# Values of both branches made ahead of the projection stream, as two stages of seven block products

## The chip, the cores and the metric

The kernel runs on one core of a Trainium2 chip. The metric is the device time of one execution in microseconds, as the median of the runs shown. All data is float32. The matrix products that matter run as three passes of the "fp32r" kind: each operand is split into a high part and a low part, and high times high, high times low and low times high are added up in PSUM. TensorE is called PE here, VectorE DVE, ScalarE ACT, GpSimd POOL, and the engine that only issues transfers SP.

## The reference

A sequence of 1024 tokens with 1024 channels goes through one layer. What is computed, cut to what matters:

```python
h = rms_norm(x, norm_w) * (1 + scale) + shift          # scale, shift from c @ ada_w
hq, hf, hi, hz, gq, gk, gv, gz, ga, mg = split(h @ w_in)
y_h = hgrn2_branch(hq, hf, hi, hz)                     # 8 heads of 128
y_g = gla_branch(gq, gk, gv, gz, ga)                   # 4 heads, keys 128, values 256
merged = sigmoid(mg0) * (y_h @ w_branch0) + sigmoid(mg1) * (y_g @ w_branch1)
out = rms_norm(x + gate * (merged @ w_out), final_norm_w)
```

Each branch is a gated linear attention in chunks: a head needs its queries, keys, per-channel decays, its values, and a gate z. The values are plain columns of the projection: `gv = h @ w_in[:, C_GV:C_GV+1024]` for the four GLA heads and `hi = h @ w_in[:, C_HI:C_HI+1024]` for the eight HGRN heads. Each of these two is a product of 1024x1024 by 1024x1024, and these two products are what the change rewrites.

## The kernel before

**Staging.** The normalised input h is made transposed, in eight pieces of 128 channels, each split into `h_hi[k]` and `h_lo[k]` (L238 to L242), and h itself is also stored to DRAM (`h_d`). A first group of products (L372, functions `products` and `first_group`) makes the four GLA queries and two of the GLA keys while the second half of h is still being made. Its transposes of x (L227) are the last readers of the tiles that hold x. Then a stream of jobs runs: each job loads one block of w_in columns through SP, splits it (the cast to the high part on ACT, L200, the subtraction for the low part on DVE, L201) and runs its products on PE.

- `Feat` (L581): 128 columns of w_in as the stationary operand, 1024 tokens moving, 48 matmuls of 512 columns. There are 34 of these jobs, for keys, queries, gates and decays.
- `Vblk` (L640 to L642): the values of one GLA head. The tokens are stationary and 256 columns of w_in move: 192 matmuls of 256 columns, four times.
- `Vblk2` (L683 to L685): the values of four HGRN heads, 512 columns moving: 192 matmuls of 512 columns, twice.

**Order of the work.** `Stream.go` runs the jobs; after each step of a job `weave` lets generators on a side track (the attention heads, one after the other) and on a back track (`prepare`, `gate_side`) write their next piece of code. A side generator yields the number of steps that it wants to wait, and PACE is what one step counts on the side track. Once the list of jobs is written this way, a scheduler orders each engine's instructions, so neighbours may change places, but each engine then executes strictly in its order. All large SBUF tiles come from 46 slots of 4 KB a partition (`Slots`); a new tile in a slot waits until the old one's readers are done, a store to DRAM among them.

**What stands around the change.** `alpha_side` makes the decays of the four GLA heads: eight small matmuls (L967) through two PSUM tiles, read by ACT (L969), then exponentials and logarithms on ACT. `factors` (L1198), on the back track, loads the stored h in blocks and makes the four differences of blocks that the later stages need, and stores them (`f_x`). `weight_sums` does the like for later weights. The later stages (`last_stages`, L1387, and `out_stage`, L1564) already multiply in blocks of a two by two split with seven products in place of eight, in the order PRODUCTS. After product 3 of the first of them, `scores_done` and `side_done` wait until the attention heads have written all their code, and take over their PSUM banks.

## Time and profile before

| what | value |
|---|---|
| median of the runs (three, 1207.8 to 1210.91) | 1208.65 us |
| span of the profiled execution (the page gives no time of its own beside it) | 1206.9 us |
| PE busy | 1184.5 us, 98% |
| PEld (weight loads, beside PE) | 988.0 us, 82% |
| DVE busy | 792.9 us, 66% |
| ACT busy | 548.6 us, 45% |
| moved by DMA | 183.51 MB, 152 GB/s over the span |
| last matmuls of the first group start | 111.69 us |
| first value matmul (L640) | 138.05 us |

A busy time is the union of an engine's instructions. Matmuls overlap each other in these records, so the mean duration of one is longer than the distance from one start to the next. The rows of groups give line, engine, operation, names, shape and count, then busy time and mean duration, then the idle time before them and what ended it. The rows of a window give for each engine its busy time and count, then the clock granted to TensorE (1.00 is full), the share of the DMA engines and GB/s.

### The profile page before, as it was taken

To read this page: it belongs to the slowest core of one execution; us is meant where nothing else is said; L and a number is where in the kernel's file an instruction comes from. 1 tells how busy PE (TensorE), PEld (TensorE's weight loads), DVE (VectorE), ACT (ScalarE), POOL (GpSimd) and SP (SyncE) were. 2 spreads that over 40 slices of the span, in tenths; PEclk is the share of its full clock that TensorE was granted. 3 is DMA by queue.
4 is the path that set the end of the run, shared out by engine and by line. 5 is a ranking of instruction groups with operands and counts; after the bars stand their busy time and mean duration, and the time that the engine had idled before them with its cause. 6 is when DMAs were issued, how large, how long until landed. Compare 5 with 4: busy or idle time off the path is not lost.

```text
span 1206.9 us, 20911 instructions
## 1 busy us (share of the span) xinstructions
PE 1184.5 (98%) x8617; PEld 988.0 (82%) x8617; DVE 792.9 (66%) x1258; ACT 548.6 (45%) x798; POOL 94.3 (8%) x204
## 2 busy tenths in 40 slices
PE   6999999999999999999999999999999999999997
PEld 5777889889798888888888888877888888878886
DVE  4737444774857557777965455795654865988994
ACT  5646732434435244234433324455743544444554
POOL 4100000101101012011100000000120000000000
PEclk8999999999999999999999999999999999999999
DMA  9814000754544167354441212154797846435423
GB/s 324 277 70 140 19 19 19 278 154 147 174 141 141 62 218 232 127 167 159 140 166 46 69 53 71 36 175 153 246 344 268 275 152 205 137 105 174 167 100 134
DMA packets 130960, 183.51 MB, mean 152 GB/s; under 512 B 7467, under 2 KB 97633, under 8 KB 130866
## 3 DMA queue, kind: packets, MB, share of 16 engines
q1 hardware_dynamic: 117250, 136.87, 36.0%
q0 software_dynamic: 13568, 45.31, 9.7%
q8 instruction: 67, 1.10, 0.4%
q14 instruction: 27, 0.22, 0.1%
q10 hardware_dynamic: 48, 0.01, 0.0%
HBM read 132.87 MB, written 49.28 MB: 151 GB/s over the span
## 4 chain that ended last, share of the span: by engine, by line
PE 71%; issue 20%; DVE 3%; ACT 2%; DMA 2%; POOL 1%; SPq 0%; POOLq 0%; DVEq 0%; ACTq 0%
PE pd L581 22%; PE pd L1387 13%; PE sc_ps L1387 6%; PE pm L1387 6%; PE pd L1564 3%; PE pd L683 2%; PE pd L684 2%; PE pd L685 2%; PE sc_ps L1564 2%; PE pm L888 2%; PE pm L890 1%; PE pm L869 1%; PE pm L1564 1%; PE sc_ps L723 1%; PE sc_ps L755 1%
## 5 line engine op out<-in xcount | busy, mean ns | idle before, releaser
L581 PE MATMUL pd<-b,b 128*128 128x512 f32 x1632 | 387.8, 394 | 0.0
L581 PEld LDWEIGHTS pd<-b,b 128*128 128x128 f32 x1632 | 302.3, 188 | 65.3 <-issue 1.4
L1387 PE MATMUL pd<-b,b 128*128 128x512 f32 x720 | 173.6, 392 | 1.9 <-DVE b L993 1.0
L1387 PEld LDWEIGHTS pd<-b,b 128*128 128x128 f32 x720 | 133.7, 188 | 32.9 <-PE pd L1387 1.4
L201 DVE TENSOR_TENSOR b<-b,b 128x1024 fp32r<-128x1024 f32 (+1 forms) x86 | 96.2, 1125 | 75.0 <-ACT b L200 59.7
L200 ACT CAST b<-b 128x1024 fp32r<-128x1024 f32 (+1 forms) x86 | 82.5, 971 | 93.2 <-PE pd L581 12.2
L1330 DVE TENSOR_TENSOR b<-b,b 128x1024 fp32r<-128x1024 f32 x56 | 68.5, 1224 | 57.0 <-ACT b L1329 37.0
L1329 ACT CAST b<-b 128x1024 fp32r<-128x1024 f32 x56 | 58.6, 1051 | 66.6 <-PE pd L1387 19.0
L1387 PE MATMUL sc_ps<-b,b 128*128 128x512 f32 x324 | 79.3, 391 | 0.3 <-ACT scT L833 0.3
L640 PE MATMUL pd<-b,b 128*128 128x256 f32 x256 | 74.2, 290 | 0.0
L642 PE MATMUL pd<-b,b 128*128 128x256 f32 x256 | 72.5, 283 | 0.0
L641 PE MATMUL pd<-b,b 128*128 128x256 f32 x256 | 72.4, 283 | 0.0
L1308 DVE TENSOR_TENSOR b<-b,b 128x1024 fp32r<-128x1024 f32 x48 | 57.8, 1222 | 21.8 <-ACT b L1307 14.5
L1387 PE MATMUL pm<-b,b 128*128 128x512 f32 x300 | 72.1, 389 | 0.0
L1387 PEld LDWEIGHTS sc_ps<-b,b 128*128 128x128 f32 x324 | 60.3, 188 | 13.9 <-ACT scT L833 0.7
L1307 ACT CAST b<-b 128x1024 fp32r<-128x1024 f32 x48 | 49.9, 1051 | 35.3 <-PE pd L1387 15.7
L1387 PEld LDWEIGHTS pm<-b,b 128*128 128x128 f32 x300 | 56.3, 188 | 11.7
L372 PE MATMUL pd<-b,b 128*128 128x512 f32 x192 | 52.3, 404 | 2.5 <-ACT b L200 1.5
L775 ACT COPY xb<-b 128x512 f32<-128x512 f32 x48 | 29.4, 620 | 50.5 <-PE sc_ps L755 25.2
L1244 POOL DMA_DIRECT2D ws<-b x64 | 34.7, 542 | 225.4 <-DVE b L1238 121.0
L683 PE MATMUL pd<-b,b 128*128 128x512 f32 x128 | 51.2, 400 | 0.0
L684 PE MATMUL pd<-b,b 128*128 128x512 f32 x128 | 50.0, 390 | 0.0
(300 smaller groups left out, 1955.0 us busy)
## 6 DMA issues: line engine op xcount, KB each, us to landing
b<-in_w_in_dram SPq DMA_DIRECT2D x66, 512.0 KB, 4.0
ws<-b POOLq DMA_DIRECT2D x64, 256.0 KB, 3.0
b<-ws SPq DMA_DIRECT2D x32, 512.0 KB, 4.3
b<-in_x_dram SPq DMA_DIRECT2D x16, 512.0 KB, 6.2
b<-in_ada_w_dram SPq DMA_DIRECT2D x32, 256.0 KB, 6.4
b<-in_w_branch_dram SPq DMA_DIRECT2D x16, 512.0 KB, 4.5
b<-h SPq DMA_DIRECT2D x14, 512.0 KB, 3.8
wo<-b POOLq DMA_DIRECT2D x14, 512.0 KB, 5.3
```

Of the source, the lines that this page charges most:

```text
L200: nc.scalar.copy(hi, src)
L201: nc.vector.tensor_sub(lo, src, hi.bitcast(F32))
L581: nc.tensor.matmul(ps[0:w, th * 512:(th + 1) * 512], a[:, k, 0:w], b[:, th * 512:(th + 1) * 512], start=(k == 0 and n == 0), stop=(k == KT ...
L640: nc.tensor.matmul(o, lh, hi[:, k % 4, :], start=(k == 0), stop=False)
L641: nc.tensor.matmul(o, lh, lo[:, k % 4, :], start=False, stop=False)
L642: nc.tensor.matmul(o, ll, hi[:, k % 4, :], start=False, stop=(k == KT - 1))
L683: nc.tensor.matmul(o, lh, hi[:, k % 2, :], start=(k == 0), stop=False)
L684: nc.tensor.matmul(o, lh, lo[:, k % 2, :], start=False, stop=False)
L1329: nc.scalar.copy(hi, t)
L1330: nc.vector.tensor_sub(lo, t, hi.bitcast(F32))
L1387: nc.tensor.matmul(o, a[:, sl], c, start=(p in (1, 5) and kt == 0 and n == 0), stop=(kt == 3 and n == 2), skip_group_check=True)
L1564: nc.tensor.matmul(o, a, b, start=(p in (1, 5) and kt == 0 and n == 0), stop=(kt == 3 and n == 2), skip_group_check=True)
```

## The change

The 1024x1024 products of the values are taken out of the stream and made right behind the first group, by a new function `front`, in two stages: first the GLA values (s = 0), then the HGRN values (s = 1). Each stage is seven block products of 512x512x512 (order 1, 2, 5, 3, 6, 7, 4), each of which runs over four tiles of 128 tokens with 12 matmuls of 512 columns a tile. The tokens are the stationary operand, the weights move. Four of the products take sums of weight blocks (`v_sums`: loaded, added on DVE, stored, loaded again), and four take the differences of h that `factors` makes, which therefore now run here and no longer on the back track. The results go to DRAM (`v_d`), and each attention head loads its own columns when it comes to its third part (`early`). The GLA queries and keys of the first group are stored too (`qk_d`) and loaded again by each head. `alpha_side` writes its eight matmuls into the first value product. The heads of the GLA branch start behind the gates, PACE is 1.3, and the weight sums start behind the value stages.

```diff
-PACE = 1.1
+PACE = 1.3
...
-        g_state[("q", f) if f < 4 else ("k", f - 4)] = qk_t[f]
...
+                    nc.gpsimd.dma_start(qk_d[f], qk_t[f])
+                    S.free(qk_t[f], sent=True)
...
-    class Vblk:
...
-    class Vblk2:
...
-    def attention(q, k, f, v, vo, V, post, lead=3):
+    def attention(q, k, f, v, V, post, early, lead=3):
...
+        early()
...
+        zs = {}
+        for h in range(4):
+            zb = zs[h] = S.get([T])
+            for th in range(2):
+                pz = mtile()
+                nc.tensor.matmul(pz, aw4[:, h * P:(h + 1) * P], ga4[:, th * 512:(th + 1) * 512],
+                                 start=True, stop=True)
+                nc.scalar.activation(zb[:, th * 512:(th + 1) * 512], pz, AF.Identity,
+                                     bias=vec[:, R_AB + h:R_AB + h + 1])
+            yield 2
+        S.free(ga4, aw4)
...
+            pair = (h0, h0 + 1)
+            for h in pair:
+                m = alphas[h] = S.get([T])
+                nc.vector.tensor_scalar_min(m, zs[h], 0.0)
+                nc.vector.scalar_tensor_tensor(zs[h], m, 2.0, zs[h], ALU.mult, ALU.subtract)
...
+        def early():
+            for i in range(2):
+                v.append(S.get([4, 256]))
+                nc.sync.dma_start(v[i], v_d[0][i * 512:(i + 1) * 512, h * 256:h * 256 + 256].rearrange(
+                    "(c p) f -> p c f", p=P))
...
+        if h < 3:
+            load_qk(h + 1)
...
+    def load_qk(h):
+        for f, key in ((h, "q"), (4 + h, "k")):
+            if f < NG:
+                t = g_state[key, h] = S.get([T])
+                nc.sync.dma_start(t, qk_d[f])
...
+        for vh in range(2):
+            def z_done(ps, h=h, vh=vh):
+                silu_done(g_state, ("z", h, vh))(ps)
+                if vh and h < 3:
+                    start_side(gla_attention(h + 1))
+            J.append(Feat(col(C_GZ + h * 256 + vh * P), rhs_h, z_done))
...
-            while len(S.free_list) < 12:
-                yield 1
...
-    stream.back.append([prepare(), 60])
...
+    def v_sums(s):
+
+        for kk in range(2):
+            y = {}
+            for at_ in ((0, 1), (1, 1), (0, 0), (1, 0)):
+                y[at_] = S.get([2, 512])
+                nc.sync.dma_start(y[at_], w_block(s, *at_, kk))
+            yield
+            e = S.get([2, 512])
+            add = nc.vector.tensor_add
+            add(e, y[0, 1], y[1, 1])
+            add(y[0, 0], y[0, 0], y[0, 1])
+            yield
+            add(y[0, 1], y[0, 0], y[1, 1])
+            nc.vector.scalar_tensor_tensor(y[1, 0], y[0, 1], -1.0, y[1, 0], ALU.mult, ALU.subtract)
+            for p, t in ((5, e), (7, y[0, 0]), (6, y[0, 1]), (3, y[1, 0])):
+                nc.gpsimd.dma_start(vs_d[s][p][kk], t.rearrange("p a f -> p (a f)"))
+            S.free(y[1, 1])
+            S.free(e, y[0, 0], y[0, 1], y[1, 0], sent=True)
+            yield
...
+    def load_vw(n):
+        if n >= len(V_SEQ):
+            return
+        s, p = V_SEQ[n]
+        vraw[n] = []
+        for kk in range(2):
+            t = S.get([2, 512])
+            if p in SUMS:
+                nc.sync.dma_start(t.rearrange("p a f -> p (a f)"), vs_d[s][p][kk])
+            else:
+                nc.sync.dma_start(t, w_block(s, *X_OF[p], kk))
+            vraw[n].append(t)
...
+    def prep_vw(n):
+        if n >= len(V_SEQ):
+            return
+        raw = vraw.pop(n)
+        vw[n] = list(zip(*[split(t) for t in raw]))
+        S.free(*raw)
...
+    def load_xf(n):
+        p = V_SEQ[n][1]
+        xraw[n] = [S.get([T]) for _ in range(2)]
+        for kk in range(2):
+            nc.sync.dma_start(xraw[n][kk], f_x[p][kk])
+
+    def build_xf(n):
+        raw = xraw.pop(n)
+        xf[n] = list(zip(*[split(t) for t in raw]))
+        S.free(*raw)
...
+        def run(self, n):
+            p = V_SEQ[n][1]
+            if p in (1, 5):
+                self.bank[BANK[p]] = RF.get()
+            o = self.bank[BANK[p]]
+            for kt in range(4):
+                x_hi, x_lo = self.x_part(n, kt)
+                w_hi, w_lo = (z[kt // 2][:, kt % 2, :] for z in vw[n])
+                for j, (a, c) in enumerate(((x_hi, w_hi), (x_hi, w_lo), (x_lo, w_hi))):
+                    nc.tensor.matmul(o, a, c, start=(p in (1, 5) and kt == 0 and j == 0),
+                                     stop=(kt == 3 and j == 2), skip_group_check=True)
+                if kt % 2:
+                    stream.weave(1)
...
+        def after(self, p):
+            bank, snap = self.bank, self.snap
+            if p == 1:
+                if self.s:
+                    self.seed()
+                else:
+                    snap[1] = self.take("a", -1.0)
+            elif p == 2:
+                self.put(0, 0, self.take("a"))
+                RF.free(bank.pop("a"))
+            elif p == 5:
+                snap[5] = self.take("e")
+            elif p == 6:
+                t = self.take("b", -1.0)
+                nc.vector.tensor_sub(t, t, bank["e"])
+                self.put(0, 1, t)
+                RF.free(bank.pop("e"))
+            elif p == 7:
+                t = snap.pop(5)
+                nc.vector.tensor_add(t, bank["b"], t)
+                self.put(1, 1, t)
+            elif p == 4:
+                self.put(1, 0, self.take("b"))
+                RF.free(bank.pop("b"))
+
+    def front():
+        vs = [v_sums(s) for s in range(2)]
+        xs = factors(h_d, f_x)
+        for i, _ in enumerate(first_group()):
+            if i == 15:
+                make_ga(1)
+            elif i in (16, 17, 18, 19, 20, 21):
+                next(vs[0])
+            elif i == 22:
+                load_vw(0)
+            stream.weave(1)
+        next(vs[0], None)
+        start_side(alpha_side())
+        lent = [dtile() for _ in range(2)]
+        RF.lend([sc_ps[:, 0:512], sc_ps[:, 512:1024]])
+        RF.lend([pd[:, i * 512:i * 512 + 512] for pd in lent[::-1] for i in range(2)])
+        next(xs)
+        prep_vw(0)
+        load_vw(1)
...
+        def pm_done():
+            while not alpha_ps[0]:
+                stream.weave(1)
+            pms.extend(mtile() for _ in range(2))
+            RF.lend(pms)
+            for i in (2, 3):
+                tiles[0, i].seed()
...
+        for n, i, steps in ((0, 1, 2), (0, 2, 3), (0, 3, 2), (1, 0, 3)):
+            on(n, i, lambda steps=steps: [next(xs, None) for _ in range(steps)])
+        for n, (s, p) in enumerate(V_SEQ):
+            on(n, 0, lambda n=n: load_vw(n + 2))
+            on(n, 1, lambda n=n: prep_vw(n + 1))
+            if p not in RAW_X:
+                on(n - 2, 3, lambda n=n: load_xf(n))
+                on(n - 1, 2, lambda n=n: build_xf(n))
+        for i in range(3):
...
+        for i in (0, 1):
+            on(2, 3, tiles[0, i].seed)
+        on(3, 1, pm_done)
...
+        on(6, 3, order_banks)
+        on(12, 1, lambda: load_qk(0))
+        on(13, 0, first_head)
+        on(13, 1, lambda: stream.ahead(0, 2, 0))
+        on(13, 3, lambda: stream.ahead(0, 2, 1))
+        for n, (s, p) in enumerate(V_SEQ):
+            for i in range(4):
+                tiles[s, i].run(n)
+                tiles[s, i].after(p)
+                for f in todo.get((n, i), ()):
+                    f()
+            for z in vw.pop(n):
+                S.free(*z)
+            for z in xf.pop(n, ()):
+                S.free(*z)
+        stream.back.append([prepare(), 4])
+        stream.back.append([gate_side(), 4])
```

Three places show how the order moves. Names are tile numbers; `b` tiles live in the 46 slots.

**SP, behind the loads of x.** Before (block columns for `Feat` and `Vblk`, then blocks of h for `factors`):

```order
L563 DMA b76_812<-in_w_in_dram 128x8x128
L563 DMA b82_986<-in_w_in_dram 128x8x128
L617 DMA b85_1064<-in_w_in_dram 128x4x256
L617 DMA b86_1066<-in_w_in_dram 128x4x256
L563 DMA b92_1140<-in_w_in_dram 128x8x128
L563 DMA b102_1224<-in_w_in_dram 128x8x128
L617 DMA b108_1438<-in_w_in_dram 128x4x256
L617 DMA b107_1436<-in_w_in_dram 128x4x256
L563 DMA b112_1548<-in_w_in_dram 128x8x128
```

Now, behind b81, b82 and b84, which are also blocks for `v_sums`:

```order
L1674 DMA b85_1047<-in_w_in_dram 128x2x512
L1674 DMA b86_1049<-in_w_in_dram 128x2x512
L1674 DMA b87_1051<-in_w_in_dram 128x2x512
L1699 DMA b89_1088<-in_w_in_dram 128x2x512
L1699 DMA b90_1090<-in_w_in_dram 128x2x512
L1111 DMA b91_1104<-h10_116 128x1024
L1111 DMA b92_1106<-h00_112 128x1024
L1111 DMA b93_1108<-h12_118 128x1024
L1699 DMA b99_1120<-in_w_in_dram 128x2x512
L1111 DMA b94_1110<-h02_114 128x1024
L1111 DMA b114_1227<-h01_113 128x1024
L1699 DMA b100_1122<-in_w_in_dram 128x2x512
```

L1674 are blocks for the weight sums, L1699 weights of the first product (b89, b90) and of the second (b99, b100), L1111 blocks of h for `factors`. b81, b82 and b84 take slots of x tiles; b91 to b93, b99 and b100 take slots of blocks and sums of `v_sums`. Where three loads of projection weights stood, there are now fifteen loads from b81 to b100.

**DVE, at the end of the first group.** Before (the low part of h, then the small lower-bound vector):

```order
L357 MEMSET pm32_975 128x512
L201 TENSOR_TENSOR b18_154<-b81_928,b10_146 128x512
L159 COPY vec_89<-pm33_988 128x22
L514 COPY lmx_698<-vec_89 128x8
L515 TENSOR_TENSOR lb_696<-vec_89,lmx_698 128x8
L517 COPY lsm_699<-lb_696 128x8
L518 RECIPROCAL lsm_699<-lsm_699 128x8
L519 TENSOR_TENSOR lb_696<-lb_696,lsm_699 128x8
```

Now:

```order
L351 TENSOR_SCALAR b70_680<-pd2_173 128x512
L1682 SCALAR_TENSOR_TENSOR b87_1051<-b84_1045,b87_1051 128x1024
L351 TENSOR_SCALAR b71_681<-pd2_173 128x512
L351 TENSOR_SCALAR b72_682<-pd3_174 128x512
L353 COPY b74_684<-sc_ps_72 128x512
L201 TENSOR_TENSOR b98_1117<-b90_1090,b97_1116 128x1024
L351 TENSOR_SCALAR b73_683<-pd3_174 128x512
L353 COPY b75_685<-sc_ps_72 128x512
L1114 TENSOR_TENSOR b92_1106<-b91_1104,b92_1106 128x1024
L1114 TENSOR_TENSOR b91_1104<-b91_1104,b93_1108 128x1024
L201 TENSOR_TENSOR b96_1113<-b89_1088,b95_1112 128x1024
L1114 TENSOR_TENSOR b93_1108<-b93_1108,b92_1106 128x1024
```

L1681 and L1682 are sums of `v_sums`, L351 and L353 take the first group's results out of PSUM, and L201 on b98 and b96 makes the low parts of the first value product's weights (from b90 and b89). The differences of h (L1114) that need b91, b92 and b93 now stand ahead of the low part b96.

**ACT, behind the first group.** Before:

```order
L363 COPY b68_658<-pm32_975 128x512
L516 ACT_TABLE_LOAD
L516 ACTIVATE lb_696<-lb_696 128x8
L969 ACTIVATE b83_1000<-pm34_1002,vec_89 128x512
L969 ACTIVATE b83_1000<-pm35_1005,vec_89 128x512
L200 CAST b89_1105<-b82_986 128x1024
L200 CAST b95_1173<-b86_1066 128x1024
L977 ACTIVATE b83_1000<-b83_1000 128x1024
L980 ACT_TABLE_LOAD
L980 ACTIVATE b83_1000<-b83_1000,ones_78 128x1024
```

Now (L882 is the former L969, L1755 takes a value product out of PSUM):

```order
L363 COPY b68_658<-pm32_993 128x512
L200 CAST b97_1116<-b90_1090 128x1024
L200 CAST b95_1112<-b89_1088 128x1024
L200 CAST b107_1192<-b99_1120 128x1024
L882 ACTIVATE b101_1142<-pm36_1143,vec_89 128x512
L200 CAST b109_1196<-b100_1122 128x1024
L882 ACTIVATE b101_1142<-pm37_1146,vec_89 128x512
L518 ACT_TABLE_LOAD
L518 ACTIVATE lb_702<-lb_702 128x8
L1755 ACTIVATE b102_1155<-pd33_1102 128x512
L882 ACTIVATE b105_1167<-pm38_1168,vec_89 128x512
L882 ACTIVATE b105_1167<-pm39_1171,vec_89 128x512
```

The four casts of the weights of the first two value products now stand ahead of and between the readers of the small matmuls: the cast that needs b100 (b109) stands ahead of the reader of the second small PSUM tile (pm37).

217 lines of the change are left out of this document (82 added, 135 removed).

## The prediction

> **What bounds the kernel now.** I read the head of the page first, then the waits of PE, then the start times of matmuls.
>
> ```profile
> span 1206.9 us, 20911 instructions
> PE 1184.5 (98%) x8617; PEld 988.0 (82%) x8617; DVE 792.9 (66%) x1258; ACT 548.6 (45%) x798; POOL 94.3 (8%) x204
> PE pm L399 <- DVE b L214: 4.6, 3, 3.5
> PE pm L158 <- DMA rows_c<-in_c_dram: 2.3, 1, 2.3
> ```
>
> PE is busy 98% of the span, and the two longest waits of PE on anyone sum to 4.6 and 2.3 us, both at the program's start. So PE sets the end everywhere, work taken from PE is worth its full length, and every wait that is put on PE costs its full length. The next question is what a matmul costs. The groups of the two value products:
>
> ```profile
> L640 PE MATMUL pd<-b,b 128*128 128x256 f32 x256 | 74.2, 290 | 0.0
> L641 PE MATMUL pd<-b,b 128*128 128x256 f32 x256 | 72.4, 283 | 0.0
> L642 PE MATMUL pd<-b,b 128*128 128x256 f32 x256 | 72.5, 283 | 0.0
> L683 PE MATMUL pd<-b,b 128*128 128x512 f32 x128 | 51.2, 400 | 0.0
> L684 PE MATMUL pd<-b,b 128*128 128x512 f32 x128 | 50.0, 390 | 0.0
> L685 PE MATMUL pd<-b,b 128*128 128x512 f32 x128 | 49.9, 390 | 0.0
> ```
>
> These 283 to 400 ns may not be added up: the records overlap. The distance from start to start decides. From the timeline, the first `Vblk` and what follows it; from the chain of waits, a run of 78 and one of 12 matmuls of 512 columns:
>
> ```profile
> 138.05 0.28 PE L640 MATMUL pd<-b,b 128*128 128x256 f32 x1
> ...
> 161.09 3.14 PE L581 MATMUL pd<-b,b 128*128 128x512 f32 x13
> 480.62 17.73 PE pd L581 x78
> 1170.30 2.72 PE pm L1564 x12
> ```
>
> 192 matmuls of 256 columns take 161.09 - 138.05 = 23.04 us, 0.120 each. 512 columns take 17.73/78 or 2.72/12, 0.227 each.
>
> **The change, part by part. What PE is spared.** Out go 768 matmuls of 256 columns, 92.2 us, and 384 of 512 columns, 87.2 us. In come 2 stages x 7 products x 4 tiles x 12 = 672 of 512 columns, 152.5 us. PE is spared 26.9 us. (The busy sums would say 370 - 263 = 107 us; they count overlap twice.)
>
> **What the value stages wait for.** The stages need blocks summed, stored and loaded again, and the differences of h made at once, where they had been made at leisure. I follow the transfers of the first stage from the moment at which they can start. SP's own waits, and PE around the end of the first group:
>
> ```profile
> SPq L563 <- PE pm L227: 37.0, 1, 37.0
> 93.32 0.60 PE L227 MATMUL pm<-ident,b 128*128 128x128 f32 x4
> ...
> 97.82 1.88 PE L967 MATMUL pm<-b,b 128*128 128x512 f32 x4
> 99.14 1.49 PE L372 MATMUL pd<-b,b 128*128 128x512 f32 x4
> ...
> 110.32 1.53 PE L581 MATMUL pd<-b,b 128*128 128x512 f32 x6
> 111.69 0.84 PE L372 MATMUL sc_ps<-b,b 128*128 128x512 f32 x3
> 112.37 1.02 PE L967 MATMUL pm<-b,b 128*128 128x512 f32 x2
> ```
>
> SP stood 37.0 us until the transposes (L227) freed the tiles of x; the last ones end at 93.9. In the new order the loads b81, b82, b84 and all behind them wait for the same transposes. So the bulk cannot start before 93.9. The first group ends at 112.37 less what is now behind it, six feature matmuls (111.69 - 110.32 = 1.37) and two of the small ones (99.14 - 97.82 = 1.32): 109.7. A small one is 0.66. If nothing waited, three products with the eight small ones would be through at 109.7 + 144 x 0.227 + 5.3 = 147.7.
>
> How fast is the DMA? Two windows in which `factors` ran before, with loads on SP's queue and stores on POOL's at once, and a median landing:
>
> ```profile
> 226.00:230.00 4.00, 4.00 (x19) 3.31 (x18) 2.57 (x5) 2.60 (x3) 0.00 (x0) 1.00 1.04 410
> 230.00:234.00 4.00, 4.00 (x19) 3.33 (x18) 2.23 (x6) 1.88 (x2) 2.16 (x4) 1.00 1.03 417
> b<-fx SPq DMA_DIRECT2D x8, 512.0 KB, 3.7
> ```
>
> The last two figures are the share of the DMA engines and GB/s: full, at 410 to 417. I take 400, so 1.31 us for 512 KB; of 3.7 us from issue to landing 2.4 are not transfer, and I count half of it, 1.2, once the queue is full. The durations on ACT and DVE:
>
> ```profile
> L200 ACT CAST b<-b 128x1024 fp32r<-128x1024 f32 x70 | 72.8, 1051 | 92.9 <-PE pd L581 12.2 <-DMA b<-in_w_in_dram 11.4 <-DVE b L1242 9.2
> L969 ACT ACTIVATE b<-pm,vec 128x512 f32<-128x512 f32 x8 | 5.3, 682 | 6.5 <-PE pm L967 6.5
> L977 ACT ACTIVATE b<-b 128x1024 f32<-128x1024 f32 x4 | 4.2, 1060 | 4.0 <-DVE b L972 3.9
> L980 ACT ACTIVATE b<-b,ones 128x1024 f32<-128x1024 f32 x4 | 4.5, 1148 | 0.0
> L984 ACT ACTIVATE b<-b 128x1024 f32<-128x1024 f32 x4 | 4.1, 1055 | 0.0
> L992 ACT ACT_TABLE_LOAD x7 | 9.0, 1283 | 0.1
> L1361 ACT ACTIVATE b<-pd 128x512 f32<-128x512 f32 x12 | 7.1, 594 | 10.8 <-PE pd L1387 10.8
> L1209 DVE TENSOR_TENSOR b<-b,b 128x1024 f32<-128x1024 f32 x8 | 9.8, 1224 | 2.4 <-DMA b<-h 2.2
> ```
>
> *First wait.* The second piece of the first product's low weights (b96) stands on DVE behind two differences that need b91, b92 and b93. On SP these are behind b81, b82, b84 to b87, b89 and b90: eleven loads. POOL has a store of sums or of first-group results ready nearly all that time, and the two queues shared the engines above, so I count eleven stores beside them: 22 x 1.31 = 28.8, landed at 93.9 + 28.8 + 1.2 = 123.9, and two DVE instructions of 1.22 behind: 126.4. PE has been idle since 109.7.
>
> *Second wait.* The small matmuls use two PSUM tiles in turn. The fourth needs the reader of the second, which on ACT stands behind the cast of b100, the fifteenth load. b100's slot must first have been stored (the last sum of `v_sums`, behind two results of the first group), so by then fifteen stores stand beside: 30 x 1.31 = 39.3, landed at 134.4. Cast and reader, 1.05 + 0.68: 136.1. PE would be there at about 132.
>
> *Third wait.* From there ACT is the bound. Up to the cast of b120, the second half of the difference of h for product 5, 33 instructions stand in its order: 6 table loads (7.7), 5 casts (5.3), 6 readers like L969 (4.1), 3 exponentials (3.2), 3 logarithms (3.4), 2 of the kind of L984 (2.1), 7 copies of half tiles like L1361 (4.2) and a tiny one (0.2): 30.1 us. The cast ends at 166.2; PE has the first two products and the small matmuls behind it by about 157. Of product 5, 42 matmuls are left: 9.5, so its end is at 175.7 in place of 147.7: 28 us late. Product 3 waits another 1 for ACT's readers of product 5. I take 29. Behind it PE needs 10.9 us a product, ACT about 7 (4 casts, 4 copies), DVE about 8, and the DMA 3 to 4 MB, 8 to 10 us: covered, closely.
>
> Bounds: at 351 GB/s (the slowest full window below) a transfer is 1.49, thirty of them 5.4 more: 34. Without any store beside the loads, 12 (worked out as the first rival).
>
> *The clock.* PE idles some 17 us in the first wait, 5 to 10 in the third. At the start of the program the clock after such a gap was:
>
> ```profile
> 12.00:14.00 2.00, 0.00 (x0) 0.00 (x0) 0.00 (x0) 1.33 (x3) 1.63 (x9) 0.91 1.03 383
> 14.00:16.00 2.00, 0.84 (x4) 0.85 (x5) 1.24 (x3) 1.97 (x6) 0.14 (x1) 0.50 1.10 351
> 18.00:20.00 2.00, 2.00 (x11) 2.00 (x11) 1.71 (x4) 0.28 (x1) 0.00 (x0) 0.50 1.10 366
> ```
>
> The third figure from the end: 0.50 from 14 to 20 us, so 3 us of work lost. Behind the first wait it is hidden, since ACT sets the pace; behind the third it is on the path: between 0 and 3, I take 1.5. The Trainium skill, "TensorE: Matmul & The Clock Gate", Part 1 on the HAM clock gate, says that one idle window of about 3.4 us halves the clock until about 3.4 us have been busy; by that page the loss would be an estimated 1.7 and the sum 0.2 longer. The trace agrees on the half clock and shows it for longer.
>
> *The rest.* 28 more low parts and 16 sums on DVE (54 us), 28 casts and 28 more readers net of the old ones on ACT lie beside the 152 us of value products. The loads of v, q and k in the heads (22 of 512 KB) lie in a stretch where DMA moved under 200 GB/s. For the heads, packed closer, and the joints between stages I take 2 us, between 0 and 20 (second rival).
>
> **Sum.** 1206.9 - 26.9 + 29 + 1.5 + 2 = 1212.5 for the profiled execution; the median of the runs stands 1.75 above its span, which gives 1214 us. Against 1208.65 that is 0.45% slower: the saved product is paid back, and a little more, between 110 and 176 us. A change under about 0.3%, 3.6 us, cannot be told from none in this kernel.
>
> **Rivals.** *The front is not starved (faster).* If the engines serve SP's loads before POOL's stores, the six loads behind 93.9 land at 103, the last sums are made by 105.4, its store goes third behind two results of the first group at 109.7, ends at 114.8, and b100 lands at 117.3, 17 earlier: the front loses 12, not 29, and the time is 1197. For it: stores beside loads at 410 GB/s did not slow anything on PE before. Against: nothing in the trace shows a preference, and the fx stores there landed later than the loads. The Trainium skill, "DMA: Bandwidth & Descriptors", section on queues, rings and completion order, says that each engine takes turns between its queues packet by packet, which speaks against this rival; no run here shows the packets.
>
> *DVE becomes the bound in the heads (slower).* Two stretches and the first score matmuls of two heads:
>
> ```profile
> 540.00:570.00 30.00, 30.00 (x366) 24.68 (x365) 23.35 (x50) 12.56 (x23) 4.34 (x8) 1.00 0.50 165
> 570.00:600.00 30.00, 30.00 (x267) 24.99 (x266) 28.76 (x52) 10.21 (x13) 4.88 (x9) 1.00 0.47 146
> 543.07 1.24 PE sc_ps L723 x64
> 588.54 1.25 PE sc_ps L723 x64
> ```
>
> DVE worked 52.1 us in 60, so 39.5 in the 45.5 of one head, weight sums included. The new order has 132 feature matmuls from head to head where 156 stood: 40.1 us. It decides once DVE needs more than that; at 1.7 us a head, twelve heads cost 20 beyond my 2: 1232. Against it: the weight sums meet only two or three HGRN heads.
>
> *The second stage starves too (slower).* Its sums are eight loads and eight stores, 21 us of transfers, between the last two products of the first stage and product 5 of the second, some 40 us later, while v is stored too. If slots hold them up, 10 us: 1224.
>
> **How the numbers follow.** Forecast 0.50, its own range 1206 to 1222, with 0.20 of it under the border of 1212.3. Rival one 0.27 (0.25 faster, 0.02 same), rival two 0.13, rival three 0.10. Faster 0.25, same 0.22, slower 0.53. The range of 1197 to 1232 leaves half of rival one out below and half of rival two above.
>
> **What would show it.** Right: PE idle from about 110 to 126, waiting for DVE at the first value product; a wait on ACT at the fourth small matmul; ACT busy without a gap until product 5; the DMA share near 1 from 94 to 155 us; then no gap of PE over 1 us up to the second stage's end, near 280 us. Wrong: the first value product running at 112, or waits of PE of several us among the score matmuls of the heads.

## The result, and the profile after

The changed kernel takes 1274.09 us (median of 4 runs, 1272.91 to 1278.22) against 1208.22 us before: a ratio of 1.0546, 95% interval 1.0528 to 1.0563. It is 5.5% slower. The forecast was 1214 us with a range of 1197 to 1232: the sign was right, the size was not. The profiled execution took 1274.5 us with a span of 1272.8; the one of before had a span of 1206.9, so 65.9 us are to be explained.

The head of the page after:

```profile
span 1272.8 us, 20397 instructions
PE 1188.4 (93%) x8137; PEld 963.1 (76%) x8137; DVE 850.5 (67%) x1318; ACT 582.1 (46%) x852; POOL 124.2 (10%) x258
```

PE was idle for 22.4 us before (1206.9 - 1184.5) and is for 84.4 us now (1272.8 - 1188.4): 62.0 us more. PE was also busy 3.9 us longer, although 26.9 us of matmuls are gone, so 30.8 us of its busy time are matmuls that took longer. Half clock explains most of that: counted over the busy time, the granted clock took away 24.9 us now and 2.7 before. The other 8.6 are not placed. 62.0 + 3.9 = 65.9. The saving was made, and more than three times as much was lost in waits and in the clock behind them.

The largest waits of PE (tile, line, whom it waited for: us in total, times, longest; one of 3.9 us at the program's start, which was there before, is left out):

```profile
PE sc_ps L670 <- DVE blk L653: 10.0, 2, 6.1
PE pm L783 <- ACT b L764: 9.4, 9, 2.0
PE sc_ps L670 <- DVE tot L673: 9.1, 4, 3.9
PE pd L372 <- DVE b L351: 8.9, 2, 7.6
PE pd L1745 <- ACT b L200: 6.5, 1, 6.5
PE pm L880 <- ACT b L882: 4.5, 1, 4.5
PE pm L1745 <- ACT b L1753: 3.2, 1, 3.2
PE sc_ps L1745 <- ACT pd L1769: 3.1, 1, 3.1
```

L670 is the second group of score matmuls of a head, L783 the matmul that reads the transposed k, L372 the first group, L880 the small matmuls, L1745 the value products. The largest waits stand in the heads, where the prediction had put 2 us. The value stages in stretches of 20 us (the last three figures are the granted clock, the share of the DMA engines and GB/s):

```profile
100.00:120.00 20.00, 10.60 (x36) 7.32 (x34) 9.67 (x11) 1.04 (x1) 4.76 (x9) 0.76 1.04 415
120.00:140.00 20.00, 8.91 (x20) 4.48 (x20) 10.55 (x14) 4.39 (x5) 4.23 (x8) 0.67 1.03 418
140.00:160.00 20.00, 17.63 (x50) 11.89 (x51) 13.84 (x19) 18.54 (x24) 1.59 (x3) 0.80 0.93 370
160.00:180.00 20.00, 18.09 (x77) 14.00 (x76) 7.61 (x9) 19.16 (x24) 2.17 (x4) 1.00 0.39 141
240.00:260.00 20.00, 17.89 (x68) 14.45 (x69) 6.63 (x6) 8.78 (x13) 2.01 (x4) 0.82 0.94 356
```

From the timeline of PE after, four borders: the first value product, the last tile of the third one (product 5), the first feature matmul, and the first matmul of the branch stage:

```profile
126.04 3.76 PE L1745 MATMUL pd<-b,b 128*128 128x512 f32 x7 [6.50 <-ACT b L200]
184.60 2.88 PE L1745 MATMUL pd<-b,b 128*128 128x512 f32 x12
320.83 1.75 PE L583 MATMUL pd<-b,b 128*128 128x512 f32 x7
863.83 2.45 PE L1293 MATMUL pd<-b,b 128*128 128x512 f32 x10
```

and the last of these borders in the timeline of before:

```profile
803.02 1.52 PE L1387 MATMUL pd<-b,b 128*128 128x512 f32 x6
```

With these the 65.9 us divide into stages. When the row at 184.60 starts, 139 value matmuls have gone (seven of them belong to the fourth product, which the scheduler moved ahead), so the 144 of three products are through at 184.60 + 5 x 0.227 = 185.7. Behind the last border there are also 30 small matmuls of the seventh HGRN head (lines L802 and L804) that stood ahead of it before: 3.2 us, which the table counts with the heads. "Predicted" are the terms of the sum on record.

| term | predicted, us | measured, us | how |
|---|---|---|---|
| matmuls spared | -26.9 | -26.9 | taken over |
| up to the end of three value products' work | +30.5 (29 and 1.5) | +38.0 | 185.7 - 147.7 |
| rest of the value stages | 0 | +13.9 | 320.8 - 185.7, less 528 matmuls of 0.227 and 64 score matmuls (1.3) |
| heads and joints | +2 | +39.0 | 863.8 - 803.0 = 60.8, less the three terms above (25.0), and the 3.2 |
| behind the heads | 0 | +1.9 | 65.9 - 60.8 - 3.2 |

One head shows what happens in them. VectorE in the fourth GLA head; its first scores began at 514.96:

```profile
513.11 0.42 DVE L961 TENSOR_TENSOR b<-b,b 128x256 f32<-128x256 f32 x1
521.08 0.69 DVE L1146 TENSOR_TENSOR b<-b,b 128x512 f32<-128x512 f32 x1 [7.55 <-DMA yg<-b]
521.69 0.68 DVE L1148 TENSOR_TENSOR b<-b,b 128x512 f32<-128x512 f32 x1
522.29 0.68 DVE L665 TENSOR_TENSOR xb<-b,tot 128x512 f32<-128x512 f32 x1
526.27 0.38 DVE L673 TENSOR_TENSOR tot<-tot 128x64 f32<-128x64 f32 x1
```

L1146 is an addition of the weight sums. It writes to a slot that still holds a result of the head before (yg), whose store has not landed. VectorE takes its instructions in order, so the chain from L665 on, which makes the operands of the second scores and takes the first ones out of PSUM, stands behind it for 7.55 us. PE runs out of feature matmuls meanwhile and waits 6.11 us. VectorE was not overloaded, it stood. The same kind of wait was there before, but shorter, and PE waited at the second scores only once, for 0.7 us; first the row of before, then the one of after:

```profile
DVE b L1239 <- DMA yg<-b: 4.2, 1, 4.2
```

```profile
DVE b L1146 <- DMA yg<-b: 13.1, 2, 7.5
```

### The profile page after: what moved, and what is told of

Read it like the earlier page. It is cut to its first block, busy times and chain, and to the rows that moved or that the text cites. A ratio compares the mean times of both kernels' runs of the same rounds, so it can differ in the third digit from the quotient of the medians.

```text
span 1272.8 us, 20397 instructions
## 1 busy us (share of the span) xinstructions
PE 1188.4 (93%) x8137; PEld 963.1 (76%) x8137; DVE 850.5 (67%) x1318; ACT 582.1 (46%) x852; POOL 124.2 (10%) x258
## 4 chain that ended last, share of the span: by engine, by line
issue 61%; PE 25%; POOL 7%; DMA 3%; DVE 2%; ACT 1%; SPq 0%; POOLq 0%; ACTq 0%; DVEq 0%
PE pd L1293 9%; PE sc_ps L1293 5%; PE pm L1293 4%; PE pd L1470 3%; POOL ws L1151 3%; PE sc_ps L1470 2%; POOL v L1760 1%; PE pm L1470 1%; DMA qk<-b 1%; POOL yh L870 1%; DMA b<-in_x_dram 1%; POOL yg L870 1%; DMA vs<-b 1%; DMA b<-in_w_in_dram 1%; PE pd L372 1%
## 5 line engine op out<-in xcount | busy, mean ns | idle before, releaser
L583 PEld LDWEIGHTS pd<-b,b 128*128 128x128 f32 x1632 | 306.0, 191 | 65.3
L201 DVE TENSOR_TENSOR b<-b,b 128x1024 fp32r<-128x1024 f32 (+1 forms) x114 | 129.8, 1148 | 128.1 <-ACT b L200 93.5
L200 ACT CAST b<-b 128x1024 fp32r<-128x1024 f32 (+1 forms) x114 | 111.1, 989 | 189.5 <-DMA b<-in_w_in_dram 54.2
L1293 PEld LDWEIGHTS pd<-b,b 128*128 128x128 f32 x720 | 133.8, 188 | 31.6 <-ACT b L1364 1.4
L1745 PE MATMUL pd<-b,b 128*128 128x512 f32 x360 | 93.0, 413 | 12.3 <-ACT b L200 6.5
L1745 PEld LDWEIGHTS pd<-b,b 128*128 128x128 f32 x360 | 69.5, 197 | 34.2 <-ACT b L200 7.2
L1293 PE MATMUL pm<-b,b 128*128 128x512 f32 x300 | 72.1, 389 | 0.0
L1293 PEld LDWEIGHTS pm<-b,b 128*128 128x128 f32 x300 | 56.3, 188 | 11.7
L372 PE MATMUL pd<-b,b 128*128 128x512 f32 x192 | 53.4, 410 | 9.7 <-DVE b L351 8.9
L372 PEld LDWEIGHTS pd<-b,b 128*128 128x128 f32 x192 | 35.1, 192 | 22.3 <-DVE b L351 10.1
L802 PE MATMUL pm<-scT,b 128*128 128x128 f32 x256 | 46.9, 275 | 0.0
L1745 PE MATMUL pm<-b,b 128*128 128x512 f32 x168 | 41.3, 396 | 3.2 <-ACT b L1753 3.2
```

What stands on the lines that cost most here:

```text
L200: nc.scalar.copy(hi, src)
L201: nc.vector.tensor_sub(lo, src, hi.bitcast(F32))
L372: nc.tensor.matmul(accs[f], wg(a, d, f), b[d][:, half * 512:half * 512 + 512], start=(d == 0 and n == 0), stop=(d == KT - 1 and n == 2))
L583: nc.tensor.matmul(ps[0:w, th * 512:(th + 1) * 512], a[:, k, 0:w], b[:, th * 512:(th + 1) * 512], start=(k == 0 and n == 0), stop=(k == KT ...
L1293: nc.tensor.matmul(o, a[:, sl], c, start=(p in (1, 5) and kt == 0 and n == 0), stop=(kt == 3 and n == 2), skip_group_check=True)
L1745: nc.tensor.matmul(o, a, c, start=(p in (1, 5) and kt == 0 and j == 0), stop=(kt == 3 and j == 2), skip_group_check=True)
```

## The experiments

Each kernel is the changed kernel with the edit shown. Ratios are to the kernel before, measured on the same chip; the changed kernel's own is 1.0546 (1.0528 to 1.0563).

### The heads

**Weight sums later.**

```diff
-        stream.back.append([prepare(), 4])
+        stream.back.append([prepare(), 100])
```

> The weight sums (additions on VectorE, lines 1145 to 1149 of the changed kernel) start 100 side units after the value stages in place of 4, so that the first three GLA heads run without them. Theory A: in the GLA heads the second score matmuls (L670) are late because VectorE, which works in order, stands on a weight sum that waits for a load or for the slot of a store (2.7, 5.5, 4.5 and 7.6 us of VectorE idle in the four heads), and PE then runs at half clock behind the gap. Without the sums the gaps of 2.6, 3.9 and 3.9 us go, with the clock behind them: per head 5 to 7 us, together 15 to 20, so 1254 to 1259 us; VectorE then has the second scores ready within 1 us. Theory B: PACE 1.3 in place of 1.1 leaves too few feature matmuls (24 in place of 30) between the two score groups, whatever VectorE does besides: the gaps keep at least two thirds of their size and the time is 1266 to 1274.

Measured: 1261.89 us, 1.0434 (1.0419 to 1.0450). In the GLA heads the second scores come 7.4, 5.6, 5.6 and 5.5 us behind the first, where they came 9.2, 9.5, 9.9 and 11.7 behind. Theory A holds for the GLA heads, and theory B falls: 5.6 us between the two groups are enough when nothing stands ahead of the chain. The gain is 3 to 8 us smaller than expected, since the sums now meet the HGRN heads. The waits of PE there, in this run:

```profile
PE sc_ps L670 <- DVE tot L673: 8.9, 3, 4.1
```

These are 1.9, 4.1 and 2.9 us in HGRN heads one to three, and the stretch behind the heads is 5.4 us longer (1258.0 - 843.6 = 414.4 in place of 409.0). Two rows of 50 us, most of it the second GLA head, after and then in this run:

```profile
376.00:426.00 50.00, 45.39 (x428) 37.26 (x427) 34.28 (x69) 16.98 (x29) 5.92 (x11) 0.93 0.44 143
```

```profile
376.00:426.00 50.00, 49.87 (x417) 41.72 (x416) 30.25 (x57) 18.45 (x31) 0.00 (x0) 1.00 0.26 75
```

VectorE (the third busy time) works 34.3 of 50 us with the sums and 30.3 without, so it was not full; PE is idle 4.6 us in the one and 0.1 in the other, and the clock is 0.93 against 1.00.

**The same sums at the same place, in other slots.**

```diff
+        S.behind = 8
         stream.back.append([prepare(), 4])
```

> The weight sums stay where the change has them; a slot that was freed by a store is only given out 8 requests later than others, from the end of the value stages on (this rule was in force only behind the heads). Theory A1 (the waits in the GLA heads come from slots that the stores of yg still hold, 5.5 and 7.6 us of VectorE in the second and fourth head): those two waits go, the second scores come 2 to 5 us earlier in heads 2 and 4, and the time falls by 5 to 10 us to 1264 to 1269. Theory A2 (it is the loads of the sums and the additions themselves, whatever slot they take): under 3 us, 1271 to 1276.

Measured: 1253.65 us, 1.0379 (1.0351 to 1.0408): 20.4 us faster than the changed kernel, by one number in the order in which slots are given out. VectorE in the second GLA head of this run:

```profile
384.38 0.69 DVE L665 TENSOR_TENSOR xb<-b,tot 128x512 f32<-128x512 f32 x1 [2.67 <-PE sc_ps L638]
388.56 0.73 DVE L1146 TENSOR_TENSOR b<-b,b 128x512 f32<-128x512 f32 x1
```

The addition L1146 now stands behind the chain, not ahead of it (the scheduler put it there, so the edit changed VectorE's order along with the slot, and the run does not tell the two apart), and in heads 2 to 4 the second scores come 5.5 to 5.6 us behind the first. Theory A1 holds, and its expected gain was too small by half: I had counted the two waits on yg, but the third head's 4.5 us, whose cause the trace did not name, went as well. The stretches of half clock went with the gaps: four in the GLA heads of the changed kernel, one here. In the first head the wait (2.8 us, for the sums' own load) stays.

**Matmuls without use in the gap.**

```diff
         yield 5
+        if me <= 4:
+            pz = mtile()
+            for _ in range(12):
+                nc.tensor.matmul(pz, h_hi[0][:, 0:P], h_hi[1][:, 0:512], start=True, stop=True)
         for b in range(32):
```

> Twelve matmuls without use (128x512, 2.7 us at full clock) stand before the second score matmuls of the four GLA heads, so that PE is idle there for 1.2 to 3.4 us in place of 2.6 to 6.1. Theory A (the gap costs twice, once as idle time and once as half clock behind it): the half clock behind the four gaps goes or shrinks, 2 to 3 us a head, and the time falls by 6 to 11 us to 1263 to 1268, although PE does 11 us more work. Theory B (the granted clock is no cost, the gaps alone are): no change, or up to 3 us slower, where the matmuls are longer than the gap.

Measured: 1276.36 us, 1.0552 (1.0537 to 1.0568), no change, as theory B had it, but not by its reason. Heads 2 to 4 took 64.5, 64.7 and 66.6 us in place of 67.5, 65.7 and 67.7, 5.1 us less, although PE did 2.7 us more in each; the first took 72.9 in place of 65.8, 4.8 of it in a new wait on VectorE's state copies. The extra matmuls take a PSUM tile out of turn, which probably made that wait; so the run does not say what the half clock costs in all. Heads 2 to 4 took 195.8 us together; in the six other runs that leave the heads as they are, they took 197.6 to 200.6. So the gain in these three heads is beyond the spread, but only by 2 to 5 us in all.

**Transposes early.**

```diff
         scoring.discard(me)
-        yield 3.5
+        yield 2.3
...
         S.free(k)
-        yield 1.5
+        yield 2.7
```

> In each head 1.2 side units are moved from ahead of the transposes of k to behind their copy (L764), so that 12 feature matmuls, as with PACE 1.1, in place of 6 lie between the copy and the matmul that reads it. Theory: the nine waits of L783 on the copy L764 (9.4 us) come from PACE 1.3, which halved the cover; they go, and the time falls by 7 to 10 us to 1264 to 1267. Rival (the copy is late because ScalarE is behind with the score copies): the waits keep their size or move to the transposes, within 3 us of 1274.

Measured: 1265.10 us, 1.0457 (1.0431 to 1.0483), 9.0 us faster. The wait L783 on L764 in this run:

```profile
PE pm L783 <- ACT b L764: 4.3, 8, 0.9
```

So 9.4 us fell to 4.3, and an HGRN head takes 40.8 us in place of 41.3. The theory holds in the main: with the cover given back the waits are halved, though they do not go. That the pace of 1.3 took the cover is read from the code; a pace of 1.1 was not run.

**Both.**

> Slots later in the heads, and transposes early: two causes in the heads at different places. If they are two, the gains of 20.6 and 9.2 add, less 1 to 2 for the head in which both counted the same stretch: 1244 to 1248 us. If the transposes waited only because of the sums' slots: 1252 to 1255.

Measured: 1256.26 us, 1.0390 (1.0368 to 1.0412). The gains do not add. The second scores come nearly as early as with the slots alone (5.6, 5.6 and 7.0 us behind the first in heads 2 to 4), but the third GLA head takes 68.6 us in place of 64.5: with the transposes early, PE waits there for VectorE's state copies (L789: 2.1 us the longest, 6.3 in six waits, against 0.8 in the changed kernel). The cover that was moved is missing at the next place.

### The value stages

How far do executions differ by themselves? Five runs above leave everything up to the heads as it is (all of "The heads"). Their value products start at 122.7 to 125.6 us, the last tile of the third at 182.0 to 183.7, and the value stages end at 317.9 to 322.4; in the changed kernel's profile it is 126.0, 184.6 and 320.8. So only differences of more than about 4 us are read below.

**Fewer transfers.** 

```diff
-                    nc.gpsimd.dma_start(qk_d[f], qk_t[f])
-                    S.free(qk_t[f], sent=True)
+                    S.free(qk_t[f])
...
-                nc.sync.dma_start(t, qk_d[f])
+                nc.sync.dma_start(t, h_d[0][f % 4])
```

> The six stores of q and k of the first group (512 KB each) are left out; the heads load the stored h in place of them, as many bytes, so q and k of six heads' halves are wrong and the rest of the work is the same. Theory A (the front waits for the transfers that share the DMA engines): six transfers of 1.31 us fewer between 113 and 126 us; the value start moves from 126.0 to 122 to 124, the fourth small matmul from 140.1 to about 132, the end of product 5 from 183 to 175 to 178, and the time falls by 5 to 8 us to 1266 to 1269. Theory B (the waits there are by ScalarE and by the order of slots, and the DMA is full but not late): under 2 us.

Measured: 1261.63 us, 1.0434 (1.0418 to 1.0449), 12.5 us faster, with 3.1 MB less in a stretch in which the engines are full. The first value product starts at 117.3 in place of 126.0, the last tile of the third at 173.1 in place of 184.6, and the stages end at 310.5 in place of 320.8. That is theory A's place, and more than its gain. But the edit does a second thing: without the stores the six tiles' slots are free at once, and in the changed kernel the cast ahead of the first value product had stood on such a slot:

```profile
124.94 1.04 ACT L200 CAST b<-b 128x1024 fp32r<-128x1024 f32 x1 [7.66 <-DMA qk<-b]
```

So the run does not tell fewer bytes from freed slots. Where slots of stores are given out later and the bytes stay (below), the value products start at 116.2 too, but the gain is gone when the stages end.

**Decay factors late.** 

```diff
         alpha_ps[0] = True
+        yield 60
```

> The exponentials, logarithms and table loads of the decay factors (some 20 us of ScalarE between 143 and 188 us) start 60 side units later, behind product 5; the eight small matmuls and their readers stay. Theory A (ScalarE sets the pace from 136 to product 5): product 5 ends 8 to 12 us earlier, at 171 to 175 in place of 183, and the time is 1262 to 1266. Theory B (the casts of product 5 wait for its operands from the DMA, full until 153 us, and for half clock on PE): product 5 ends 2 to 5 us earlier, and the time is 1269 to 1273.

Measured: 1272.06 us, 1.0512 (1.0495 to 1.0530): 2 us, with intervals that overlap. From the timeline of PE in this run, the last tile of the third product, and one of the second stage:

```profile
174.69 2.98 PE L1746 MATMUL pd<-b,b 128*128 128x512 f32 x12
235.87 4.37 PE L1746 MATMUL sc_ps<-b,b 128*128 128x512 f32 x11 [9.05 <-ACT pd L1770]
```

174.7 in place of 184.6: ScalarE was the bound there, as theory A and the prediction had it. But theory A's time did not come: the gain is given back at 227 to 236, in one wait of 9.05 us.

**Raw weights first.** In `front`, the loads and splits of the first two products go ahead of the sums:

```diff
-            elif i in (16, 17, 18, 19, 20, 21):
-                next(vs[0])
-            elif i == 22:
-                load_vw(0)
+            elif i == 16:
+                load_vw(0)
+            elif i == 17:
+                load_vw(1)
+            elif i == 18:
+                next(vs[0])
             stream.weave(1)
-        next(vs[0], None)
+        prep_vw(0)
+        for _ in vs[0]:
+            pass
...
-        prep_vw(0)
-        load_vw(1)
```

> The weights of the first two value products, which need no sums, are loaded and split ahead of the sums; the same transfers, in another order, and the sums' additions stand behind the first group on VectorE. Theory A (the transfers as a whole set the third product, and the order only says where PE waits): the value start moves from 126 to 110 to 114, the gap in the first group (7.6 us) goes, and a wait of 8 to 16 us appears at the third product, whose end stays within 4 us of 183; the time falls by 0 to 5 us, 1269 to 1274. Theory B (each operand is awaited by itself): the third product ends 8 to 13 us earlier, at 170 to 175, and the time is 1261 to 1266.

Measured: 1266.03 us, 1.0481 (1.0453 to 1.0509), 8 us faster, between the two expectations. The value products start at 109.6, which is the time that the prediction had for a front in which nothing waits. Waits of 7.7 and 4.7 us stand up to the third product, as theory A had it, but its last tile starts at 171.5, 13 us earlier, as theory B had it. When the stages end, at 318.9, 2 us of the 13 are left; the profiled execution is 3.6 us shorter than the changed kernel's, so the rest of the 8 us is not to be placed.

**Matmuls without use in the front.** 

```diff
         lent = [dtile() for _ in range(2)]
+        for _ in range(30):
+            nc.tensor.matmul(lent[0][:, 0:512], h_hi[0][:, 0:P], h_hi[1][:, 0:512], start=True, stop=True)
```

> Thirty matmuls without use (6.8 us at full clock, 13.6 at half) stand between the first group and the first value product of the changed kernel, where PE waits 6.5 us. Theory A (ScalarE sets the pace up to the third product, so the half clock behind the first wait is hidden): the first products run nearer to full clock, but the third product still ends at 181 to 186 us and the time stays within 4 us of 1274. Theory B (the half clock is on the path): the second product ends at 162 to 166 in place of 170, the third 3 us earlier, 1268 to 1271.

Measured: 1277.23 us, 1.0561 (1.0524 to 1.0597), no change. The clock from 120 to 124, after and in this run:

```profile
120.00:124.00 4.00, 0.00 (x0) 0.00 (x0) 2.75 (x5) 0.00 (x0) 2.11 (x4) 0.50 1.03 421
```

```profile
120.00:124.00 4.00, 4.00 (x19) 3.04 (x17) 2.19 (x2) 1.05 (x1) 0.87 (x2) 1.00 1.03 418
```

The clock is full where it was half, and the way to the last tile of the third product is as long: 123.7 to 182.0, against 126.0 to 184.6. Theory A holds: the half clock behind the first wait was hidden, as the prediction said.

**Sums of the second stage early**, and decay factors late.

```diff
-        for i in range(3):
-            on(6, i, lambda: [next(vs[1], None) for _ in range(3 if i else 1)])
+        for n, i, steps in ((5, 1, 1), (5, 3, 3), (6, 1, 3)):
+            on(n, i, lambda steps=steps: [next(vs[1], None) for _ in range(steps)])
```

> The decay factors are late as in the run before with that edit, which freed 10 us up to product 5 and lost 8 of them to a wait of 9.0 us at the first products of the second stage; here the sums of the second stage's weights also start one product earlier. Theory A (the second stage waits for its own sums: eight loads, eight stores and their loads): the wait of 9.0 us goes, the second stage ends at 305 to 308 in place of 316, and the time is 1261 to 1265. Theory B (the transfers as a whole are late there too): the wait moves to the last products of the first stage, and the time stays at 1268 to 1273.

Measured: 1272.48 us, 1.0530 (1.0509 to 1.0550), no change. The wait of 9 us is gone, and 2.7, 1.6, 2.2, 1.4 and 4.0 us stand at other value products between 202 and 251. Theory B.

**No sums in the second stage.** 

```diff
-        vs = [v_sums(s) for s in range(2)]
+        vs = [v_sums(0), iter(())]
...
-                nc.sync.dma_start(t.rearrange("p a f -> p (a f)"), vs_d[s][p][kk])
+                nc.sync.dma_start(t.rearrange("p a f -> p (a f)"), vs_d[0][p][kk])
```

> The sums of the second stage's weights are left out (eight loads, eight stores of 512 KB, eight additions); the second stage loads the first stage's sums in their place, so HGRN's values are wrong and all else is the same as in the changed kernel. Theory A (the second stage waits for its sums): the waits of 3.3 and 3.1 us at 233 and 239 and the half clock behind them go, the fifth product of the second stage (480th matmul) comes at 260 to 265 in place of 273, and the time is 1255 to 1265. Theory B (the stores of v, the factors and the other loads are late there as well): under 4 us, over 1270.

Measured: 1271.31 us, 1.0521 (1.0496 to 1.0547), no clear change: theory A falls. The 480th value matmul came at 270.3, in place of 270.6 to 274.1 in the runs that leave this part as it is. ScalarE in this run, and SP's waits between 185 and 250 us:

```profile
230.39 1.05 ACT L200 CAST b<-b 128x1024 fp32r<-128x1024 f32 x1 [7.88 <-DMA b<-in_w_in_dram]
```

```profile
SPq L1713 <- DMA v<-b: 17.2, 2, 11.1
SPq L1699 <- DMA v<-b: 9.7, 2, 5.3
```

Without the sums, ScalarE still stands 7.9 us on a cast whose load is late, with the copies behind it that PE needs; and SP still stands 27 us on slots that the stores of v hold, and 20 more on slots whose tiles PE has yet to read. What the second stage waits for is not its sums alone.

**Slots of stores later in the value stages too.** The line `S.behind = 8` stands at the start of `front`.

> The rule on the slots of stores (given out 8 requests later) holds from the end of the first group on, not only in the heads. Theory A (in the value stages, too, loads and casts wait for slots that stores still hold, and ScalarE, which works in order, then keeps PE from its banks): the second stage ends 5 to 12 us earlier than with the rule in the heads alone (319.5), and the time is 1242 to 1249. Theory B (in the value stages the transfers and the additions themselves are late, whatever the slot): within 3 us of the run with the rule in the heads alone, 1251 to 1257.

Measured: 1253.70 us, 1.0373 (1.0356 to 1.0390), the same as with that rule in the heads alone. The value products start at 116.2, 10 us earlier, the last tile of the third at 178.6, 6 us earlier, and the stages end at 324.3, no earlier; a wait of 9.7 us stands at 236. Theory B: another order of slots only moves the wait.

**Two feature products first.** 

```diff
+                if vh and 0 < h < 3:
...
+                for job in J[:2]:
+                    job.load()
...
         start_side(alpha_side())
+        next(xs)
+        for job in J[:2]:
+            job.prep()
+        prep_vw(0)
+        load_vw(1)
+        for job in J[:2]:
+            for _ in job.run():
+                stream.weave(1)
+        del J[:2]
...
+            start_side(gla_attention(1))
```

> Two feature products (z of the first GLA head, 96 matmuls, 21.8 us of PE) are moved from the heads to the place between the first group and the value stages; nothing else. In every run so far the 480th value matmul (product 5 of the second stage) came at 270 to 273 us, whatever was done ahead of it. Theory A (the front is set by its transfers, and PE's waits there are room for other work): the waits between 119 and 245 us fall by 12 us or more, the 480th value matmul stays within 6 us of 273, and the time falls by 15 to 22 us to 1252 to 1259. Theory B (a chain through ScalarE, VectorE and PE sets it, which starts with the value stages): the chain starts 22 us later, the 480th comes at 285 or later, and the time falls by under 8 us.

Measured: 1274.57 us, 1.0546 (1.0530 to 1.0562), no change: theory B. The 480th value matmul came at 294.6. ("In every run so far" in the expectation was not so: with fewer transfers it had come at 262.7.) ScalarE is why; two rows of windows (the fourth busy time is ScalarE's), and a value product:

```profile
144.00:148.00 4.00, 4.00 (x19) 3.33 (x18) 0.90 (x2) 3.97 (x5) 0.00 (x0) 1.00 0.03 5
160.00:164.00 4.00, 0.00 (x0) 0.00 (x0) 0.74 (x1) 3.97 (x4) 0.00 (x0) 0.83 0.86 303
```

```profile
165.58 4.59 PE L1745 MATMUL pd<-b,b 128*128 128x512 f32 x11 [7.18 <-ACT b L1755]
```

The DMA was nearly idle at 144 (5 GB/s); ScalarE was full, with the decay factors and now the features' sigmoids, and the value products waited for its copies.

### Together

The next five combine the edits above.

> Together: two feature products first, the weights of the first two value products ahead of the sums, the slots of stores given out later, and the transposes early. The causes lie at different places (94 to 250 us; the GLA heads; every head), so their gains add: 20.6 by the slots, 9.2 by the transposes of which 2 to 3 lie in the first group of gains too, and what the run with two features alone gives, 15 to 22: 1226 to 1236 us. If the gains share a cause, under 30 us in all, over 1244.

Measured: 1266.68 us, 1.0476 (1.0459 to 1.0494). It is the case of "over 1244": the gains do not add, and the run is 10 us slower than slots and transposes alone (1256.26).

> As the run with the edits together, with four feature products (43.6 us of PE) ahead of the value stages. Theory A (room for other work is left between 119 and 270 us after two features, some 10 to 18 us of idle time and half clock): 8 to 15 us below the run with two, 1212 to 1226. Rival (after two features PE sets the pace of the front, or the slots that the four results hold delay its loads): within 4 us of the run with two.

Measured: 1280.07 us, 1.0604 (1.0572 to 1.0635). Neither expectation: two more features cost 13 us. Features ahead of the value stages are a loss also with the other edits.

> Slots of stores later from the first group on, transposes early, decay factors late. ScalarE was the bound up to product 5 (10 us), and that gain was lost behind at the second stage. Theory A (lost to slots): here it is kept, 1230 to 1240 us. Theory B (lost to the transfers and sums of the second stage): within 4 us of the run with slots and transposes alone.

Measured: 1267.74 us, 1.0477 (1.0445 to 1.0509), 11 us worse than slots and transposes alone, so neither theory: waits of 10.8 and 6.6 us stand in the second stage, and its end is at 333.

> As the run before it, with the raw weights first as well, which by itself gave 8 us. If each cause is one of its own: 1222 to 1234 us; if the second stage sets the end of the front whatever is ahead of it: within 3 us of the run without it. In both cases it stays above the kernel before, since the second stage's transfers remain.

Measured: 1248.47 us, 1.0330 (1.0307 to 1.0352), the fastest of all, 19 us below the run before it, between the two expectations. The last tile of the third product starts at 163.3, 21 us earlier than in the changed kernel; the stages end at 314.1, of which 7 us are left. At 212 PE waits 9.2 us for ScalarE, which stands 8.9 us on a decay factor behind VectorE, which stands on a load of the second stage's sums.

> As the run of slots, alpha and raw weights together, with the decay factors 35 side units later in place of 60, so that they lie between the third product and the sums of the second stage. In that run ScalarE stood 8.9 us on a decay factor that waited for VectorE, which stood on the second stage's sums, and PE waited 9.2 us. Theory A (that meeting is the wait): the 9.2 us shrink to 2 to 4 and the time is 1238 to 1244. Theory B (the sums are late by themselves): within 3 us of 1248.

Measured: 1251.31 us, 1.0354 (1.0333 to 1.0375). That wait went, and waits of 5.8, 3.0 and 6.1 us came at 179, 209 and 226: theory B. No version beats the kernel before.

## Why the prediction was wrong

**What bounds the kernel** was right: PE sets the end, so what is taken from it counts and every wait put on it counts in full.

**The front** was nearly right, with some luck. The value stage was to start at 126.4 and started at 126.04, and the load that the forecast of it hung on (b93) landed at 123.6, forecast 123.9. But PE's row at 126.04 names ScalarE, not VectorE: the cast of the high part had waited for the slot of a first-group result (the row at 124.94 above), which the prediction did not have, and the two waits happened to end within 1 us of each other. Nor was PE idle from 109.7 on: the first group itself stood for 7.6 and 1.4 us, because VectorE had the sums of `v_sums`, whose loads were late, ahead of the reader of its PSUM tile, and it ended at 119.5:

```profile
113.58 1.65 PE L372 MATMUL pd<-b,b 128*128 128x512 f32 x3 [7.56 <-DVE b L351]
110.44 1.23 DVE L1679 TENSOR_TENSOR b<-b,b 128x1024 f32<-128x1024 f32 x1 [2.33 <-DMA b<-in_w_in_dram]
```

The fourth small matmul was to wait for ScalarE until 136.1 and went at 140.1; ScalarE was busy 18.5 and 19.2 of 20 us up to the third product; the DMA's share was 1.04, 1.03 and 0.93 in the three windows from 100 to 160. The run that cut ScalarE's work (10 us at the third product) confirms that bound; the run that cut the stores (12.5 us) agrees with the bound by transfers, but freed slots too. The rival in which loads go ahead of stores had the load on which the fourth small matmul hangs (b100) land at 117.3; its cast, in the timeline of ScalarE after:

```profile
138.39 1.04 ACT L200 CAST b<-b 128x1024 fp32r<-128x1024 f32 x1 [5.50 <-DMA b<-in_w_in_dram]
```

It waited for the load until 138.4, 4 us later than even the forecast (134.4), so that rival falls. The Trainium skill, "DMA: Bandwidth & Descriptors", section on queues, rings and completion order, had spoken against it, and the trace agrees by the 138.4. The rival also had the last sums made by 105.4; the row at 110.44 shows an addition for them that still waited for its load. Part of b100's delay is that SP issued it only at 126.2, behind slots that stores held. The work of three products was through at 185.7, not at 175.7 + 1.5: 8.5 us more, of which 4 stood already at this cast and the others are waits on ScalarE's copies behind it (2.3 and 2.0 us the longest).

**The step "behind it ... covered, closely" failed**: the rest of the value stages lost 13.9 us. DMA, ScalarE and VectorE were each counted against PE by their busy times, product by product. What decides is that a cast or an addition whose load is late holds the PSUM copies queued behind it. Rival three had this at one place with 10 us and a chance of 0.10; its cause, the sums, was wrong by the run without them. The "near 280 us" for the end of the second stage also contradicts the prediction's own sum, 109.7 + 5.3 + 152.5 + 30.5 = 298.0; it was 320.8.

**The step that failed most is "for the heads, packed closer, and the joints between stages I take 2 us, between 0 and 20"**. It measured 39.0, with 1.9 more behind the heads. Rival two looked at the right engine and the right place, and was worked out from the wrong quantity: 39.5 us of VectorE's work against a period of 40.1. VectorE was busy 30 to 38 of 50 us in the GLA heads (320 to 520 us). It lost the time standing ahead of a chain on which PE waits, for a slot that a store still held. "The weight sums meet only two or three HGRN heads" was true and beside the point: in the new order they start with the first GLA head. By the runs, the slots cost 20.4 us and the pace at the transposes up to 9, but the two do not add. With the slots later, the heads (320.8 to 863.8 in the changed kernel, 322.4 to 843.8 there) are 21.6 us shorter, so some 17 of the 39 us are not attributed. The smaller cover between the two score groups (8.3 us before, 5.6 where nothing stands now) may be the other half of the same wait; the new order with a pace of 1.1 was not tried, so its share is only argued.

**The range** let one rival happen at a time. Losses came at the places of both two and three, by other causes than theirs. Even together they make only 1214 + 18 + 10 = 1242: the heads lost 37 us beyond the 2 where rival two had 18, and the rest of the value stages 13.9 where rival three had 10.

What sets the end of the value stages stays open in part. Shown is that leaving out six stores is worth 12.5 us, by their 3.1 MB or their slots. Shown not to be enough are the second stage's sums alone, a later order of the stores' slots alone, and the start alone. Every edit of the order gave most of its gain at the third product back by the end of the stages, the best one 14 of 21 us; only the run without the stores kept it (11.5 us at the third product, 10.3 at the end). More slots, or a longer lead of the loads, were not tried.

## What to carry to other kernels

Work taken off the engine that sets the end is a gain only if the stretch in which it is taken has slack on all others: this change put work on the DMA, ScalarE and VectorE in the value stages, left less cover in the heads, and lost more than three times the saving. An engine that works in order is judged not by its busy share but by what can stand ahead of the chain that the bound engine waits for; look for an instruction whose slot or load comes late. Where slots are handed out in turn, try handing out late those that a store still holds: that single number was worth 20 us in the heads, and nothing in the value stages.
